# Both output projections of a two-layer decoder trunk as seven half-size products

## The chip, the core and the metric

The kernel runs on one core of a Trainium2 chip. The metric is the device time of one execution in microseconds; the kernel before takes 640.55 us (median of three runs, 639.79 to 640.93). The core has a matrix engine (TensorE, PE in the profile), three engines for elementwise work (VectorE, ScalarE, GpSimd; DVE, ACT and POOL), a queue engine that only issues transfers here (SyncE, SP), a working memory of 128 partitions (SBUF) and eight banks for matmul results (PSUM).

## What is computed

The input x is 512 rows of 1024 numbers, all in float32. Two layers follow one another:

```python
# layer 0: x + mixed @ w_out_e,  mixed = [A(h) * silu(z_A) | B(h) * silu(z_B)],  h = RMSNorm(x)
# layer 1: x + mixed @ w_out_o,  mixed = [C(h) * silu(z_C) | D(h) * silu(z_D)]
mixed = jnp.concatenate([oc.reshape(B, S, C_W) * jax.nn.silu(cz),
                         od.reshape(B, S, D_W) * jax.nn.silu(dz)], axis=-1)
return x + mixed @ w_out
```

A, B, C and D are four kinds of attention with 512 output columns each; q, k, v and z come from one input projection per layer. The output projection is a product of 512x1024 by 1024x1024, and it is this product, once per layer, that is changed.

## The kernel before

Precision: a float32 product is made of three passes of rounded float32 (`F32R`). Each operand is split into a high part (a cast) and a low part (operand minus high part); the passes are high x high, high x low and low x high, and they accumulate in PSUM. So each operand costs one cast and one subtraction ahead of its matmuls.

Weights stream from DRAM in chunks of 256 rows by up to 512 columns (`Weights`, lines 355 to 419): `load` brings a chunk into a `wr` buffer (4 of them), `conv` splits it into `wh` and `wl` (3 each). ScalarE casts the high part; the low part goes to VectorE for chunks of odd number and to GpSimd, in two halves, for even ones. The order of the chunks is the list `chunks` (lines 447 to 470). When a chunk is used up, `done` converts the one three places on and loads the one five places on.

`stream` (line 473) runs one projection: four PSUM banks of tag `proj` (there are four in all), eight K-steps of 128 taken from four chunks. `out_proj` (line 793) is such a stream for the output projection: for each half of the columns, four row blocks of 128, eight K-steps and three passes, 96 matmuls of 128x512, 192 a layer. Its left operand are the gated attention outputs `MA` and `MB`: `gate` makes silu(z) from the z projection (`bz`, `az`, `cz`, `dz`), `gated` multiplies with the attention output `OT` and splits the result into two parts. Layer 0 starts with B's half (K-steps 4 to 7), so that A's last heads and gates may come later; layer 1 starts with C's half. Behind layer 0's projection each row block is added to x, transposed on TensorE and split into the next layer's `hH` and `hL` (`h_block`, line 587), and stored for the residual. The first column half supplies K-steps 0 to 3 of layer 1's first projection, `cqk0`, the second one 4 to 7. Behind layer 1's the sum is stored.

The order of the instructions is worked out ahead of time. The body is recorded as a list of operations; `Plan.schedule` (line 227) places them one by one, always the one that can start soonest by its table of prices, and among those that can start alike the one recorded first, with an advance for operations on `proj` banks (280 places) and on `wr` buffers (230 places) (`key`, line 330). Each tag has a fixed number of buffers (`TAGS`, line 28), given out in the order of recording except for the small ones. Each engine then runs its own list in that order. All transfers of weights, of K copies (`k<-k`) and of results stand in the one queue of SyncE. The planner charges a VectorE operation with two SBUF inputs up to 0.25 us if GpSimd is at work (`SHARED`, line 108). In every stage the projections of the next group serve as filler between the attention's matmuls.

Every operation is emitted by one line (352), so the profile's groups are told apart by tiles: `proj<-wh,k` and `proj<-wl,k` are the output projections' matmuls (`MA` and `MB` lie in `k` buffers, and the weights are the moving operand), `wl<-wr,wh` a weight chunk's low part, `v<-proj,v` the addition to the residual, `hL` the low part of the next layer's input.

## Time and profile before

| what | value |
|---|---|
| median of three runs | 640.55 us |
| profiled execution | 639.81 us, span 638.0 us |
| TensorE busy | 626.2 us (98%) |
| VectorE / ScalarE / GpSimd busy | 444.2 / 379.9 / 292.8 us |
| granted TensorE clock | 1.00 in all stretches |
| DRAM and SBUF transfers | 63.01 MB, mean 99 GB/s |

The span runs from the first to the last instruction. Busy time of TensorE counts matmuls that overlap in its pipeline, so the spacing of matmuls, not their length, says what one costs. Layer 0's output projection lies at 255.6 to 302 us, layer 1's ends the kernel. Times in the rows are us from the span's start unless marked ns; a row's name is output<-inputs.

### The profile page before, as it was taken

To read this page: it belongs to the slowest core of one execution; us is meant where nothing else is said; L and a number is where in the kernel's file an instruction comes from. 1 tells how busy PE (TensorE), PEld (TensorE's weight loads), DVE (VectorE), ACT (ScalarE), POOL (GpSimd) and SP (SyncE) were. 2 spreads that over 40 slices of the span, in tenths; PEclk is the share of its full clock that TensorE was granted. 3 is DMA by queue.
4 is the path that set the end of the run, shared out by engine and by line. 5 is a ranking of instruction groups with operands and counts; after the bars stand their busy time and mean duration, and the time that the engine had idled before them with its cause. 6 is when DMAs were issued, how large, how long until landed. Compare 5 with 4: busy or idle time off the path is not lost.

```text
span 638.0 us, 10566 instructions
## 1 busy us (share of the span) xinstructions
PE 626.2 (98%) x3425; PEld 526.7 (83%) x3425; DVE 444.2 (70%) x1156; ACT 379.9 (60%) x919; POOL 292.8 (46%) x406
## 2 busy tenths in 40 slices
PE   8999999999999999999999999999999999999997
PEld 7788887888888778888887788889998887887786
DVE  4674786987867894652459267688698789898631
ACT  6664785857756664453453266578578677576510
POOL 2543474753374442311363234765478454544310
PEclk9999999999999999999999999999999999999999
DMA  8553215133107123353245431152442102101321
GB/s 290 195 133 99 72 42 154 43 120 101 67 34 228 37 87 112 100 165 99 72 136 156 130 85 36 38 143 62 130 124 75 35 34 83 67 4 64 124 108 66
DMA packets 48126, 63.01 MB, mean 99 GB/s; under 512 B 4664, under 2 KB 29640, under 8 KB 48072
## 3 DMA queue, kind: packets, MB, share of 16 engines
q1 hardware_dynamic: 47896, 62.28, 32.1%
q8 instruction: 27, 0.44, 0.3%
q14 instruction: 27, 0.22, 0.1%
q10 hardware_dynamic: 176, 0.07, 0.1%
HBM read 50.80 MB, written 4.19 MB: 86 GB/s over the span
## 4 chain that ended last, share of the span: by engine, by line
PE 82%; DVE 9%; ACT 3%; issue 2%; DMA 2%; POOL 1%; SPq 0%; DVEq 0%; ACTq 0%; POOLq 0%
PE proj L352 59%; PE tr L352 10%; PE av L352 7%; PE sc L352 6%; DVE p L352 2%; DVE ptl L352 1%; DVE kn L352 1%; DMA wr<-in_w_in_e_dram 1%; DVE k L352 1%; DVE wl L352 1%; DVE sm L352 1%; ACT wh L352 1%; ACT p L352 1%; DMA wr<-in_phi_w_dram 1%; DVE sq L352 1%
## 5 line engine op out<-in xcount | busy, mean ns | idle before, releaser
L352 POOL TENSOR_TENSOR wl<-wr,wh 128x512 fp32r<-128x512 f32 (+2 forms) x87 | 103.3, 1206 | 145.4 <-ACT wh L352 145.2
L352 PE MATMUL proj<-wh,hH 128*128 128x512 f32 (+2 forms) x416 | 152.7, 369 | 1.6 <-DVE kn L352 1.0
L352 PE MATMUL proj<-wl,hH 128*128 128x512 f32 (+2 forms) x416 | 151.8, 366 | 0.0
L352 PE MATMUL proj<-wh,hL 128*128 128x512 f32 (+2 forms) x416 | 150.8, 366 | 0.0
L352 ACT ACTIVATE p<-p,sm 128x128 f32<-128x128 f32 (+3 forms) x160 | 90.0, 563 | 50.0 <-DVE sm L352 46.8
L352 ACT CAST wh<-wr 128x1024 fp32r<-128x1024 f32 (+2 forms) x89 | 83.9, 944 | 55.8 <-PE proj L352 47.4
L352 PEld LDWEIGHTS proj<-wh,hH 128*128 128x128 f32 x416 | 78.3, 189 | 13.0 <-ACT p L352 1.3
L352 PEld LDWEIGHTS proj<-wl,hH 128*128 128x128 f32 x416 | 78.5, 189 | 9.3
L352 PEld LDWEIGHTS proj<-wh,hL 128*128 128x128 f32 x416 | 78.2, 189 | 9.4
L352 PE MATMUL proj<-wh,k 128*128 128x512 f32 x256 | 83.4, 398 | 0.0
L352 DVE CUSTOM_DVE_ANT_0 p<-sc,bias 128x128 f32<-128x128 f32 (+3 forms) x160 | 76.6, 480 | 8.4 <-PE sc L352 5.5
L352 PE MATMUL sc<-k,qq 128*128 128x256 f32 (+3 forms) x304 | 79.3, 338 | 0.9 <-DVE sm L352 0.8
L352 POOL TENSOR_SCALAR p<-p,sm 128x128 f32<-128x128 f32 (+1 forms) x80 | 45.4, 570 | 71.5 <-DVE sm L352 60.6
L352 DVE TENSOR_TENSOR ptl<-tr,pth 128x128 fp32r<-128x128 f32 (+3 forms) x144 | 68.1, 484 | 11.8 <-ACT pth L352 10.3
L352 ACT CAST pth<-tr 128x128 fp32r<-128x128 f32 (+3 forms) x144 | 58.8, 421 | 27.7 <-PE tr L352 26.5
L352 POOL TENSOR_SCALAR p<-p,sm,dg 128x128 f32<-128x128 f32 (+3 forms) x64 | 44.4, 697 | 51.6 <-DVE sm L352 43.5
L352 DVE TENSOR_TENSOR wl<-wr,wh 128x1024 fp32r<-128x1024 f32 (+2 forms) x45 | 51.2, 1138 | 23.4 <-ACT wh L352 23.2
L352 PE MATMUL tr<-ident,p 128*128 128x128 f32 x360 | 62.2, 275 | 1.8 <-POOL p L352 1.2
L352 POOL TENSOR_TENSOR sm<-sm,nhalf 128x8 f32<-128x8 f32 (+3 forms) x53 | 61.9, 1169 | 3.1
L352 PEld LDWEIGHTS sc<-k,qq 128*128 128x128 f32 x304 | 51.4, 189 | 10.6 <-DVE sm L352 3.6
L352 PE MATMUL proj<-hH,wh 128*128 128x512 f32 x144 | 58.5, 407 | 0.4 <-DVE kn L352 0.4
L352 PE MATMUL proj<-hH,wl 128*128 128x512 f32 x144 | 57.7, 401 | 0.0
(148 smaller groups left out, 1103.2 us busy)
## 6 DMA issues: line engine op xcount, KB each, us to landing
wr<-in_w_in_e_dram SPq DMA_DIRECT2D x32, 256.0 KB, 2.8
wr<-in_w_in_e_dram SPq DMA_DIRECT2D x16, 512.0 KB, 4.6
wr<-in_w_in_o_dram SPq DMA_DIRECT2D x28, 256.0 KB, 2.9
k<-k SPq DMA_DIRECT2D x24, 256.0 KB, 3.3
wr<-in_w_in_o_dram SPq DMA_DIRECT2D x12, 512.0 KB, 4.1
wr<-in_w_out_e_dram SPq DMA_DIRECT2D x8, 512.0 KB, 3.6
wr<-in_w_out_o_dram SPq DMA_DIRECT2D x8, 512.0 KB, 3.9
v<-in_x_dram SPq DMA_DIRECT2D x2, 1024.0 KB
```

What stands on the lines that cost most here:

```text
L352: getattr(getattr(self.nc, op.eng), op.method)(*[real(a) for a in op.args], **{k: real(a) for k, a in op.kw.items()})
```

## The change

Each output projection is split into quarters: the left operand (the gated outputs) by row half and K half into A11, A12, A21, A22 (the first index is the row half of 256, the second the K half of 512; K's first half is B's in layer 0, C's in layer 1), the weights into four quarters of 512x512. Seven products of 256x512 by 512x512 (P0 to P6) replace the eight, in the form with S1 = A21 + A22, S2 = S1 - A11, S3 = A11 - A21, S4 = A12 - S2 on the left and four combinations of the weight quarters on the right.

The weight combinations are made by GpSimd (`combinations`): for each layer eight pieces, each with four loads of 128 KB into the one `vc` buffer, four additions or subtractions of 128x256, and four stores to a DRAM tensor (`dram0`, `dram1`). They are recorded behind the first group of B heads. The weight stream then has 14 chunks per projection instead of eight, three products' from `w_out` itself and four from the combinations.

The left operands are split per product (`split_rows`): casts on ScalarE, low parts on VectorE for five products and on GpSimd for S4 and A22. The gates now only multiply into `OT` in place. P3 adds onto P0's two banks and P5 onto P4's; P2 and P6 use the `sc` and `av` banks. Each result is added by VectorE to the two column halves of x to which it belongs (`add`), 20 additions of 128x512 a layer instead of eight, with the last addition of a block followed by `h_block` (layer 0) or the store (layer 1). `cqk0` takes its K-steps in the order 4 to 7, 0 to 3.

```diff
...
         name, pieces, q = self.order[s]
         raw = self.plan.tile("wr", [128, 2, 512])
         c = 0
+        if callable(pieces):
+            self.Y.dma_start(raw, pieces(q))
+            pieces, c = (), 512
...
+    def seven(name, w, wt, late):
+        src = w.rearrange("(kt p) c -> p kt c", p=128)
+        def quarter(k, n):
+            k = 4 * (k ^ late)
+            return lambda u: src[:, k + 2 * u:k + 2 * u + 2, 512 * n:512 * n + 512]
+        def comb(t):
+            return lambda u: wt[:, t, 2 * u:2 * u + 2, :]
+        ops = (quarter(0, 0), comb(2), quarter(1, 0), comb(1), comb(0), quarter(1, 1), comb(3))
+        return [(f"{name}P{n}", op, (0, 1)) for n, op in enumerate(ops)]
+    oeT = st("dram0", [128, 4, 4, 512])
+    ooT = st("dram1", [128, 4, 4, 512])
...
-        ("oe0", [(woe, 0, 512, 1, 0)], QO),
-        ("oe1", [(woe, 512, 512, 1, 0)], QO),
-        ("cqk0", [(wo, 0, 256, 2, 512)], Q4),
+        *seven("oe", woe, oeT, True),
+        ("cqk0", [(wo, 0, 256, 2, 512)], QO),
...
-        ("oo0", [(woo, 0, 512, 1, 0)], Q4),
-        ("oo1", [(woo, 512, 512, 1, 0)], Q4),
+        *seven("oo", woo, ooT, False),
...
+    def combinations(w, wt, late):
+        src = w.rearrange("(kt p) c -> p kt c", p=128)
+        for t in range(4):
+            for c in range(2):
+                b = st("vc", [128, 4, 256])
+                for n in range(4):
+                    kt = t + 4 * ((n // 2) ^ late)
+                    c0 = 512 * (n % 2) + 256 * c
+                    Y.dma_start(b[:, n, :], src[:, kt, c0:c0 + 256])
+                for dst, x, y, op, to in ((3, 3, 1, OP.subtract, 2), (1, 1, 0, OP.subtract, 0), (0, 3, 0, OP.add, 1),
+                                          (2, 0, 2, OP.subtract, 3)):
+                    G.tensor_tensor(out=b[:, dst, :], in0=b[:, x, :], in1=b[:, y, :], op=op)
+                    Y.dma_start(wt[:, to, t, 256 * c:256 * c + 256], b[:, dst, :])
+    def split_rows(dst, src, eng):
+        for c, v in enumerate(src):
+            A.copy(dst[0][:, 2 * c:2 * c + 2, :].bitcast(F32R), v)
+        for c, v in enumerate(src):
+            eng.tensor_sub(dst[1][:, 2 * c:2 * c + 2, :].bitcast(F32R), v, dst[0][:, 2 * c:2 * c + 2, :])
+        return dst
+    def combine(dst, a, b, op):
+        for d, x, y in zip(dst, a, b):
+            V.tensor_tensor(out=d, in0=x, in1=y, op=op)
+        return dst
+    def rows2(tag):
+        return [st(tag, [128, 512]).rearrange("p (c q) -> p c q", c=2) for _ in range(2)]
+    def parts(tag):
+        t = st(tag, [128, 2, 2, 4, 256])
+        return [(t[:, n, 0], t[:, n, 1]) for n in range(2)]
+    def two_parts():
+        return st("pth", [128, 4, 256]), st("ptl", [128, 4, 256])
+    def product(name, banks, rows, fresh=True):
+        for u in range(2):
+            _, wh, wl = W.next(name)
+            for r in range(2):
+                for kk in range(2):
+                    for pi, (w, low) in enumerate(((wh, 0), (wl, 0), (wh, 1))):
+                        T.matmul(banks[r], rows[low][:, 2 * u + kk, 128 * r:128 * r + 128].bitcast(F32R), w[:, kk, :],
+                                 start=fresh and u == 0 and kk == 0 and pi == 0, stop=u == 1 and kk == 1 and pi == 2,
+                                 skip_group_check=not fresh)
+            W.done()
+        return banks
+    def seven_products(name, OT, first, gate_first, gate_second, xs, done):
+        second = 4 - first
+        quad = [[[OT[:, k + 2 * c:k + 2 * c + 2, 256 * r:256 * r + 256] for c in range(2)] for k in (first, second)]
+                for r in range(2)]
+        (A11, A12), (A21, A22) = quad
+        def add(banks, hf, i0, op=OP.add, last=False):
+            for r in range(2):
+                V.tensor_tensor(out=xs[hf][:, i0 + r, :], in0=xs[hf][:, i0 + r, :], in1=banks[r], op=op)
+                if last:
+                    done(i0 + r, hf)
+        def two():
+            return [pt("proj") for _ in range(2)]
+        gate_first()
+        pa11, ps3 = parts("k")
+        split_rows(pa11, A11, V)
+        S3 = combine(rows2("kn"), A11, A21, OP.subtract)
+        split_rows(ps3, S3, V)
+        main = product(name + "P0", two(), pa11)
+        add(main, 0, 0)
+        side = product(name + "P1", two(), ps3)
+        add(side, 0, 2)
+        add(side, 1, 2)
+        gate_second()
+        pa12, ps2 = parts("k")
+        split_rows(pa12, A12, V)
+        S1 = combine(rows2("p"), A21, A22, OP.add)
+        S2 = combine(rows2("p"), S1, A11, OP.subtract)
+        split_rows(ps2, S2, V)
+        p2 = product(name + "P2", [pt("sc"), pt("av")], pa12)
+        ps1 = split_rows(two_parts(), S1, V)
+        add(p2, 0, 0, last=True)
+        product(name + "P3", main, ps2, False)
+        add(main, 1, 2)
+        add(main, 1, 0)
+        add(main, 0, 2)
+        S4 = combine(A11, A12, S2, OP.subtract)
+        side = product(name + "P4", two(), ps1)
+        add(side, 1, 2, last=True)
+        ps4 = split_rows(two_parts(), S4, G)
+        product(name + "P5", side, ps4, False)
+        a22 = st("qq", [128, 2, 4, 256])
+        pa22 = split_rows((a22[:, 0], a22[:, 1]), A22, G)
+        add(side, 1, 0, last=True)
+        p4 = product(name + "P6", [pt("sc"), pt("av")], pa22)
+        add(p4, 0, 2, OP.subtract, last=True)
...
+    combinations(woe, oeT, 1)
+    combinations(woo, ooT, 0)
...
-    acc = proj("bz", hH, hL, 512, True)
-    MB = new_m()
-    gate_now(acc, rb, OT, 4, MB)
-    acc = proj("az", hH, hL, 512, True)
-    gA = gate_later(acc, rb, "qq")
-    MA = new_m()
-    for a in range(4):
-        gated(gA[:, a, :], OT, a, MA)
+    def gate_b():
+        acc = proj("bz", *h0, 512, True)
+        for a in range(4):
+            g = st("sq", [128, 512])
+            gate(acc[a], rb, g)
+            V.tensor_tensor(out=OT[:, 4 + a, :], in0=g, in1=OT[:, 4 + a, :], op=OP.mult)
+        acc = proj("az", *h0, 512, True)
+        gA.append(gate_later(acc, rb, "qq"))
+
+    def gate_a():
+        for a in range(4):
+            V.tensor_tensor(out=OT[:, a, :], in0=gA[0][:, a, :], in1=OT[:, a, :], op=OP.mult)
+
+    def block_done(i, hf):
+        x1 = xs[hf]
+        h_block(x1[:, i, :], i, 4 * hf, gO, hH, hL)
+        sq = st("sq", [128, 512])
+        A.activation(out=sq, in_=x1[:, i, :], func=AF.Square, accum_out=ssh[:, hf, i:i + 1])
+        Y.dma_start(x1d[:, i, hf, :], x1[:, i, :])
     x1d = st("dram", [128, NB, 2, 512])
     ssh = st("ssh", [128, 2, NB])
+    gA, xs = [], []
+    for hf in range(2):
+        xs.append(st("v", [128, NB, 512]))
+        Y.dma_start(xs[hf], x2.rearrange("(i p) c -> p i c", p=128)[:, :, 512 * hf:512 * hf + 512])
+    h0 = hH, hL
     hH, hL = new_h()
-    for hf in range(2):
-        x1 = st("v", [128, NB, 512])
-        Y.dma_start(x1, x2.rearrange("(i p) c -> p i c", p=128)[:, :, 512 * hf:512 * hf + 512])
-        acc = out_proj(f"oe{hf}", MA, MB)
-        for i in range(NB):
-            V.tensor_tensor(out=x1[:, i, :], in0=acc[i], in1=x1[:, i, :], op=OP.add)
-            h_block(x1[:, i, :], i, 4 * hf, gO, hH, hL)
-            sq = st("sq", [128, 512])
-            A.activation(out=sq, in_=x1[:, i, :], func=AF.Square, accum_out=ssh[:, hf, i:i + 1])
-            Y.dma_start(x1d[:, i, hf, :], x1[:, i, :])
+    seven_products("oe", OT, 4, gate_b, gate_a, xs, block_done)
...
-    acc = proj("cz", hH, hL, 512, True)
-    MA = new_m()
-    gate_now(acc, rb, OT, 0, MA)
-    acc = proj("dz", hH, hL, 512, True)
-    gB = gate_later(acc, rb, "v")
-    MB = new_m()
-    for a in range(4):
-        gated(gB[:, a, :], OT, 4 + a, MB)
+    def gate_c():
+        acc = proj("cz", hH, hL, 512, True)
+        for a in range(4):
+            g = st("sq", [128, 512])
+            gate(acc[a], rb, g)
+            V.tensor_tensor(out=OT[:, a, :], in0=g, in1=OT[:, a, :], op=OP.mult)
+        acc = proj("dz", hH, hL, 512, True)
+        gB.append(gate_later(acc, rb, "qq"))
+
+    def gate_d():
+        for a in range(4):
+            V.tensor_tensor(out=OT[:, 4 + a, :], in0=gB[0][:, a, :], in1=OT[:, 4 + a, :], op=OP.mult)
+
+    def store(i, hf):
+        Y.dma_start(out[0, 128 * i:128 * i + 128, 512 * hf:512 * hf + 512], xs[hf][:, i, :])
+
+    gB, xs = [], []
     for hf in range(2):
-        xr = st("v", [128, NB, 512])
-        Y.dma_start(xr, x1d[:, :, hf, :])
-        acc = out_proj(f"oo{hf}", MA, MB)
-        for i in range(NB):
-            V.tensor_tensor(out=xr[:, i, :], in0=acc[i], in1=xr[:, i, :], op=OP.add)
-            Y.dma_start(out[0, 128 * i:128 * i + 128, 512 * hf:512 * hf + 512], xr[:, i, :])
+        xs.append(st("v", [128, NB, 512]))
+        Y.dma_start(xs[hf], x1d[:, :, hf, :])
+    seven_products("oo", OT, 0, gate_c, gate_d, xs, store)
```

## Rows read from the trace of the kernel before

**Rows 1.** The page's first part: the span, and each engine's busy time.
```profile
span 638.0 us, 10566 instructions
...
PE 626.2 (98%) x3425; PEld 526.7 (83%) x3425; DVE 444.2 (70%) x1156; ACT 379.9 (60%) x919; POOL 292.8 (46%) x406
```

**Rows 2.** The page's chain that ended last, by engine and by line.
```profile
PE 82%; DVE 9%; ACT 3%; issue 2%; DMA 2%; POOL 1%; SPq 0%; DVEq 0%; ACTq 0%; POOLq 0%
PE proj L352 59%; PE tr L352 10%; PE av L352 7%; PE sc L352 6%; DVE p L352 2%; DVE ptl L352 1%; DVE kn L352 1%; DMA wr<-in_w_in_e_dram 1%; DVE k L352 1%; DVE wl L352 1%; DVE sm L352 1%; ACT wh L352 1%; ACT p L352 1%; DMA wr<-in_phi_w_dram 1%; DVE sq L352 1%
```

**Rows 3.** Stages: length, then PE, PEld, DVE, ACT, POOL busy, clock, DMA share, GB/s.
```profile
247.50:255.60 8.10, 8.10 (x37) 6.61 (x37) 4.89 (x8) 3.09 (x5) 0.00 (x0) 1.00 0.56 194
255.60:266.60 11.00, 11.00 (x49) 9.00 (x48) 10.31 (x12) 5.11 (x7) 3.00 (x2) 1.00 0.30 99
266.60:277.60 11.00, 11.00 (x48) 8.84 (x47) 2.08 (x3) 4.07 (x8) 2.54 (x2) 1.00 0.51 165
277.60:290.00 12.40, 12.40 (x64) 10.27 (x63) 7.47 (x19) 7.17 (x21) 2.55 (x2) 1.00 0.43 130
290.00:301.90 11.90, 11.90 (x53) 9.58 (x52) 2.21 (x4) 4.19 (x8) 2.55 (x2) 1.00 0.32 109
...
540.00:600.00 60.00, 59.17 (x335) 49.71 (x333) 52.85 (x151) 41.35 (x106) 26.80 (x35) 1.00 0.14 45
600.60:634.30 33.70, 33.63 (x145) 26.70 (x143) 9.91 (x12) 4.35 (x5) 4.88 (x4) 1.00 0.32 117
```

**Rows 4.** The chain in order of time, its last long piece: start, us, what.
```profile
604.20 30.08 PE proj L352 x129
```

**Rows 5.** Groups of TensorE by shape: count, busy us, mean ns, idle before.
```profile
L352 PE MATMUL proj<-wh,k 128*128 128x512 f32 x256 | 83.4, 398 | 0.0
...
L352 PE MATMUL proj<-wl,k 128*128 128x512 f32 x128 | 50.5, 395 | 0.0
```

**Rows 6.** Timeline of TensorE where the heads end: start, us, what.
```profile
246.70 0.28 PE L352 MATMUL av<-ptl,v 128*128 128x128 f32 x1
...
255.58 0.39 PE L352 MATMUL proj<-wh,k 128*128 128x512 f32 x1
...
600.58 0.39 PE L352 MATMUL proj<-wh,k 128*128 128x512 f32 x1
```

**Rows 7.** Timeline of VectorE in layer 0's output projection.
```profile
255.56 1.23 DVE L352 TENSOR_TENSOR wl<-wr,wh 128x1024 fp32r<-128x1024 f32 x1 [0.45 <-ACT wh L352]
256.70 0.69 DVE L352 TENSOR_TENSOR kn<-proj,rb 128x512 f32<-128x512 f32 x1
257.30 1.45 DVE L352 TENSOR_TENSOR kn<-qq,ot 128x512 f32<-128x512 f32 x1
258.68 1.78 DVE L352 SCALAR_TENSOR_TENSOR qq<-qq,kn 128x512 f32<-128x512 f32 x1
...
269.63 0.69 DVE L352 TENSOR_TENSOR v<-proj,v 128x512 f32<-128x512 f32 x1 [3.64 <-PE proj L352]
...
280.15 2.16 DVE L352 SCALAR_TENSOR_TENSOR hL<-tr,lncol,hH 128x128 fp32r<-128x128 f32 x8 [0.56 <-ACT hH L352]
```

**Rows 8.** Timeline of GpSimd in the same stretch.
```profile
256.91 3.00 POOL L352 TENSOR_TENSOR wl<-wr,wh 128x512 fp32r<-128x512 f32 x2 [10.22 <-ACT wh L352]
268.01 2.54 POOL L352 TENSOR_TENSOR wl<-wr,wh 128x512 fp32r<-128x512 f32 x2 [8.10 <-ACT wh L352]
```

**Rows 9.** Timeline of ScalarE in the same stretch.
```profile
262.83 1.05 ACT L352 CAST wh<-wr 128x1024 fp32r<-128x1024 f32 x1
264.29 0.62 ACT L352 CAST k<-kn 128x512 fp32r<-128x512 f32 x1 [0.41 <-DVE kn L352]
```

**Rows 10.** The page's DMA issues: count, KB each, median us to landing.
```profile
wr<-in_w_out_e_dram SPq DMA_DIRECT2D x8, 512.0 KB, 3.6
...
wr<-in_w_in_o_dram SPq DMA_DIRECT2D x16, 128.0 KB, 2.2
```

**Rows 11.** Groups of GpSimd by shape: count, busy us, mean ns, idle before.
```profile
L352 POOL TENSOR_TENSOR wl<-wr,wh 128x256 fp32r<-128x256 f32 x16 | 11.9, 766 | 14.1 <-ACT wh L352 14.1
```

More of the change, by code (lines that the diff above doesn't have):

```diff
@@ L27 @@
 LOOSE = ("tr", "sm1", "sm2", "sm4", "sm8", "sm16", "sm64")
-TAGS = {"proj": 4, "sc": 1, "tr": 2, "av": 1, "dram": 1,
+TAGS = {"proj": 4, "sc": 1, "tr": 2, "av": 1, "dram": 1, "dram0": 1, "dram1": 1,
         "wr": 4, "wh": 3, "wl": 3, "qq": 2, "k": 2, "v": 2, "pth": 2, "ptl": 2, "hH": 1, "hL": 1, "ot": 1,
@@ L198, in price @@
             out = writes[0] if writes else reads[0]
-            local = writes and reads and all(r.root.tag not in ("dram",) for r in (writes[0], reads[0]))
+            local = writes and reads and all(not r.root.tag.startswith("dram") for r in (writes[0], reads[0]))
             rate = 270.0 if local else 330.0 if out.shape[-1] >= 256 else 180.0
@@ L340, in emit @@
     def emit(self, order, sb, ps, dr):
-        pools = {"dram": dr}
+        pools = {t: dr for t in ("dram", "dram0", "dram1")}
         pools.update({t: ps for t in PSUM_TAGS})
```

## The prediction

> **What bounds the kernel now.** I read the page's first part, then the chain of waits, then the table of stages, and last the timelines of each engine at the two output projections. The first part shows TensorE busy 626.2 of 638.0 us [rows 1]; the chain that ended last is 82% TensorE, 59% of the span being matmuls into `proj` [rows 2]. So a matmul less is worth its spacing, as long as the others can still feed TensorE. The stage table says where they can: in the four windows of layer 0's projection (255.6 to 301.9) VectorE is busy 10.31 + 2.08 + 7.47 + 2.21 = 22.1 of 46.3 us and the granted clock is 1.00; in the 60 us before layer 1's projection VectorE is busy 52.85 of 60 us; in the last 33.7 us only 9.91 [rows 3].
>
> **What is removed.** The spacing of these matmuls is in the chain's last long piece: 129 in 30.08 us, 0.233 us each; the window 255.6 to 266.6 has 49 in 11.00 us [rows 3, 4]. I take 0.23. The projections are 256 + 128 = 384 matmuls [rows 5], 192 a layer. Seven products of 2 K-steps x 2 row blocks x 2 x 3 = 24 make 168. Removed: 2 x 24 x 0.23 = 11.0 us, all on the path if nothing new waits.
>
> **What is added in layer 0.** The last attention matmul there is at 246.70 and the first projection matmul at 255.58 [rows 6]: from 246.7 on TensorE has only `az`, then the products, so no other work covers a stall until `cqk0`. Seven products last 168 x 0.23 = 38.6 us, 5.5 each. Prices on VectorE, as start to start: a 128x512 operation 0.60 (256.70 to 257.30), a weight chunk's low part 1.14 (255.56 to 256.70), an `hL` piece 2.16/8 = 0.27 [rows 7]. Each product eats two weight chunks, so VectorE makes one low part per product. Its demand, product by product:
> P0: last `az` block 3, S3 and its low part 4 (S3's `kn` buffers come free only behind the `az` gates): 7 x 0.60 + 1.14 = 5.3.
> P1: P0's additions 2, A12's low part 2, S1 and S2 4: 8 x 0.60 + 1.14 = 5.9.
> P2: P1's additions 4, low parts of S2 and S1 4: 5.9.
> P3: P2's additions 2, S4 2, `hL` 8 x 0.27: 4 x 0.60 + 2.2 + 1.14 = 5.7.
> P4: P3's additions 6: 4.7. P5 and P6: additions 2 and `hL` 8 each: 4.5.
> Sum 36.5 of 38.6 us, against 22.1 of 46.3 now. It fits only just, and up to P3 it does not: 22.8 asked of 22.1. P3 waits for S2's low part, which comes last of its queue; what queues behind it is P1's additions, which P4's banks wait for. If every operation came at its price the stall would be under 1 us.
> It will not. GpSimd makes the other low parts, and while it did so from 256.91 to 259.91 (3.00 us for two against 2.54 at 268.01) [rows 8], VectorE's two operations with both inputs in SBUF took 1.45 and 1.78 us instead of 0.69, 1.85 more together; an addition from PSUM stayed at 0.69 [rows 7]. The new stage has 7 such GpSimd pairs and 4 single low parts (S4 and A22), nine pairs in all. If a third of them meet VectorE's two-input work, as they do now only where VectorE is dense, that is 9 x 1.85 / 3 = 5.6 us more: 36.5 + 5.6 - 38.6 = 3.5 us of stall. Bounds: 0, since the additions can drift later than the combinations, and 9 x 1.85 + 36.5 - 38.6 = 14.6 if all meet. I take 3.5, near the row of dense work.
> The Trainium skill (SBUF — State Buffer, Who interferes with whom) says that a VectorE instruction with two SBUF inputs and a GpSimd instruction reading SBUF exclude one another, whoever started first keeping the port for the whole instruction, and that one with a single SBUF input is not touched. The trace agrees on both halves (1.78 against 0.69, and 0.69). Taken as the price of every pair it makes the slow rival below.
> ScalarE: 14 weight casts of 1.05 and 14 half-row copies of 0.62 [rows 9] are 23.4 us beside the squares and `hH` that it has already; no term. Weights: 512 KB per 2.75 us; one lands in 3.6 us [rows 10] and loads are issued five chunks, 13 us, ahead; no term, bounds 0 to 2.
> P5 adds onto P4's banks, so it waits for P4's additions; the first bank is complete six matmuls (1.4 us) before the second, an addition takes 0.69, so this only just hides. No term, bounds 0 to 1.4. At the end `cqk0` starts with the half that P4 and P5 complete; P6 (5.5 us) covers that `hL`, and 48 matmuls (11 us) cover the last rows. Nothing.
>
> **What is added in layer 1.** The first matmul after the last D head is at 600.58 [rows 6], and 145 matmuls follow from there [rows 3]: 47 of the 48 that need only C's half were already used as filler among the heads. There is no filler left over, so what delays the last head delays the end. VectorE, 88% busy there, gets 6 operations (low parts of A11 and S3, and S3) and 4 additions (P0, half of P1), and loses 7 low parts: +3 x 0.60, and one weight low part of 1.14: 2.9 us. Bounds: 0 (it idles 7 us in that window [rows 3]) and 6 (with every pair met). I take 2.5, since VectorE is nearly full. After the last head P2 to P6 are 120 matmuls, 27.6 us, against 13 operations, 16 additions and 4 low parts, 29 x 0.60 + 4.6 = 22 us: no term, bounds 0 to 3. The residual's second half now loads alone once the last V buffer is free and is wanted only by P4's banks, 11 us later.
>
> **The combinations.** 64 GpSimd additions and subtractions of 128x256; the like row takes 766 ns [rows 11]: 49 us, in 16 groups, one buffer, each of four loads (128 KB: 2.2 us [rows 10]), four chained operations, four stores. By these rows a group is some 2.2 + 4 x 0.77 + a store like the load, 7.5 us, an estimate of 10 with queueing: 160 us, while layer 0's are wanted at 255. They sit among the layer-0 heads. Cover: the 8.9 us of `az` that now run after the last head, which would move forward as filler. SyncE's queue gets 128 more DMAs, the stores waiting for GpSimd with weight loads and K copies behind them. The first groups' loads also fall into the start, where the weight loads are. Bounds 0 to 3; I take 0.5, nearer to the covered end because of those 8.9 us.
>
> **Sum.** 11.0 - 3.5 - 2.5 - 0.5 = 4.5 us less than the profiled execution's 639.81, which is 0.74 under the median 640.55: 636.0 on the median.
>
> **Rivals.**
> A, nothing new waits: stalls of 0 to 2 us, 630 to 631.5. For it: VectorE's 36.5 us fit, and the order is worked out ahead of time. Against it: P0 to P3 are over full even without contention.
> B, the forecast, 631.5 to 639.2.
> C, VectorE takes over as the bound of the layer-0 stage and eats all: stalls of 9.5 to 12 us, 639 to 641.8. It needs about two thirds of the pairs to meet.
> D, the shared port, on the other side: every GpSimd pair costs VectorE its 1.85 us. Layer 0's stage is then 36.5 + 16.7 = 53 us, less some 3 that may slide under `cqk0`, 50 against the 192 x 0.23 = 44.2 now: 6 us lost; in layer 1's end 22 + 6 x 1.85 = 33 against 27.6, so 5.5 - 5.5 = 0, and the heads' 2.5. 640.55 + 8.5 = 649. It decides from 11 us of stall. Against it: VectorE's additions, 20 of a layer's operations, read one SBUF operand and do not meet.
> E, the combinations come late, or their stores block SyncE's queue ahead of weight loads: only if a group took 28 us; that is not seen in any row, and I put it into D's chance.
>
> **Chances.** A 0.17, B 0.55, C 0.13, D and E 0.15. Two runs of this kernel differ by some 0.2%, 1.3 us, so faster means under 639.3: A and B, 0.72; same 0.12; slower 0.16. The range leaves out 0.08 at the bottom and about 0.12 at the top: 630.5 to 642.5; the forecast alone, 631.5 to 639.2.
>
> **What would show it.** 336 matmuls instead of 384 at 0.23 us; TensorE idle of some 3 to 4 us between P0 and P4 of layer 0 with VectorE as what ended it; VectorE over 85% busy there, two-input operations at 1 us and more; the last D head 2 to 3 us later relative to TensorE's matmuls before it; GpSimd's 64 at about 0.77 us and done well before 250 us. Wrong if the idle stands at `wh` or `wl` (weights too late), at a DMA, or at the start of the kernel; or if TensorE stays gapless and the time falls by 10.

## The result and the profile after

The changed kernel takes 657.56 us (median of four runs, 656.40 to 658.99) against 640.26 for the kernel before, now also of four runs: a ratio of 1.0273, 95% interval 1.0257 to 1.0289. Forecast were 636.0 and a range up to 642.5. The prediction was wrong, and in direction too: 17.3 us lost where 4.5 were to be won.

The profiled execution took 656.59 us. Its page: the span, busy times, and the chain that ended last by engine and by line.
```profile
span 654.6 us, 10944 instructions
...
PE 627.3 (96%) x3377; PEld 516.7 (79%) x3377; DVE 493.0 (75%) x1206; ACT 399.5 (61%) x943; POOL 382.2 (58%) x490
...
PE 47%; DVE 14%; POOL 13%; issue 6%; DMA 4%; ACT 4%; SPq 1%; POOLq 0%; DVEq 0%; ACTq 0%
```
48 matmuls are gone, as planned (3425 to 3377 [rows 1]). But the chain that was 82% TensorE [rows 2] is now 47%, and GpSimd, 1% of it before, has 13%.

The heads of layer 0 before (columns as in [rows 3]).
```profile
20.00:255.58 235.58, 233.89 (x1211) 192.78 (x1210) 175.97 (x464) 150.76 (x366) 118.63 (x165) 1.00 0.32 99
```
The stages of the changed kernel: the heads of layer 0, the products of layer 0 up to `cqk0`'s first matmul, the end of layer 1 behind the last D head, and three short stretches inside them.
```profile
20.00:265.64 245.64, 238.92 (x1212) 190.65 (x1211) 183.10 (x463) 151.97 (x367) 173.90 (x231) 1.00 0.52 164
...
265.64:316.83 51.19, 45.13 (x197) 34.76 (x196) 47.20 (x72) 31.71 (x65) 28.26 (x18) 0.97 0.53 170
...
265.64:276.00 10.36, 8.40 (x34) 5.77 (x32) 10.36 (x10) 5.11 (x7) 7.90 (x5) 1.00 0.34 104
...
278.00:280.00 2.00, 2.00 (x6) 1.59 (x5) 2.00 (x5) 1.14 (x2) 0.13 (x1) 0.50 0.68 231
...
616.00:654.60 38.60, 31.44 (x122) 23.26 (x121) 26.06 (x31) 11.75 (x16) 15.42 (x11) 0.94 0.41 136
624.00:626.00 2.00, 2.00 (x6) 1.52 (x6) 1.97 (x5) 0.00 (x0) 0.00 (x0) 0.52 0.29 75
```
VectorE is busy 7.1 us more among the heads with about the same operations (183.10 against 175.97). In layer 0's projection, where it was busy 22.1 us before [rows 3], it is busy 47.20 of 51.19 us, and at the stage's start without a gap (10.36 of 10.36).

TensorE's timeline at the products: the last layer-0 head, the first product matmul, and its longer waits, with what ended them.
```profile
256.75 0.28 PE L352 MATMUL av<-ptl,v 128*128 128x128 f32 x1
...
265.64 0.39 PE L352 MATMUL proj<-wh,k 128*128 128x512 f32 x1
...
277.29 0.85 PE L352 MATMUL proj<-wh,k 128*128 128x512 f32 x2 [2.38 <-DVE k L352]
...
287.39 0.50 PE L352 MATMUL proj<-wl,k 128*128 128x512 f32 x1 [1.08 <-POOL wl L352]
...
290.78 0.73 PE L352 MATMUL proj<-wh,k 128*128 128x512 f32 x2 [0.32 <-DVE k L352]
...
303.47 0.66 PE L352 MATMUL tr<-ident,v 128*128 128x128 f32 x4 [1.40 <-DVE v L352]
...
622.39 1.15 PE L352 MATMUL sc<-wh,k 128*128 128x512 f32 x2 [1.24 <-DVE k L352]
```

VectorE in the same stretch, and GpSimd beside it.
```profile
268.45 1.78 DVE L352 TENSOR_TENSOR kn<-ot 128x512 f32<-128x512 f32 x1
270.15 1.78 DVE L352 SCALAR_TENSOR_TENSOR qq<-qq,kn 128x512 f32<-128x512 f32 x1
271.85 0.68 DVE L352 TENSOR_TENSOR ot<-qq,ot 128x512 f32<-128x512 f32 x1
272.46 0.68 DVE L352 TENSOR_TENSOR v<-v,proj 128x512 f32<-128x512 f32 x1
273.05 1.91 DVE L352 TENSOR_TENSOR wl<-wr,wh 128x1024 fp32r<-128x1024 f32 x1
274.89 0.67 DVE L352 TENSOR_TENSOR v<-v,proj 128x512 f32<-128x512 f32 x1
275.49 1.15 DVE L352 TENSOR_TENSOR kn<-ot 128x512 f32<-128x512 f32 x1
276.56 1.45 DVE L352 TENSOR_TENSOR k<-kn,k 128x512 fp32r<-128x512 f32 x2
...
287.80 2.32 DVE L352 TENSOR_TENSOR wl<-wr,wh 128x1024 fp32r<-128x1024 f32 x1
```
```profile
267.48 3.90 POOL L352 TENSOR_TENSOR wl<-wr,wh 128x512 fp32r<-128x512 f32 x2 [1.23 <-ACT wh L352]
...
272.61 3.49 POOL L352 TENSOR_TENSOR wl<-wr,wh 128x512 fp32r<-128x512 f32 x2 [1.23 <-ACT wh L352]
```
Read the two side by side. While GpSimd works on a weight chunk (267.48 to 271.38), VectorE's operations with both inputs in SBUF take 1.78 us instead of 0.68; between two such chunks (271.85) they take 0.68; the addition from a PSUM bank takes 0.67 also in the middle of a chunk (274.89); and GpSimd's pair itself takes 3.90 and 3.49 instead of 2.54 [rows 8].

The longest wait, 2.38 us, is P1's. It is for S3's low part: S3 lies in `kn` buffers, its second half is summed at 275.49, and `k<-kn,k` at 276.56 is the subtraction that releases TensorE. P3 waits only 0.32 us for S2's low part (290.78), after 1.08 us for a weight chunk's low part (287.39).

Four marks split the span: the first product (or projection) matmul, `cqk0`'s first, the last D head's matmul, and the end. Before they stand at 255.58, 302.63, 599.96 and 638.0, after at 265.64, 316.83, 615.71 and 654.6, so the pieces are 255.58, 47.05, 297.33 and 38.04 us before and 265.64, 51.19, 298.88 and 38.89 after. The losses are 10.06 among layer 0's heads, 4.14 in its products, 1.55 in layer 1's heads and 0.85 at the end: 16.6, the difference of the spans. As each set of products has 24 matmuls less, 5.5 us, the second and the fourth take 9.6 and 6.4 us more than the matmuls left in them would need at the old pace.

### The profile page after: what moved, and what is told of

It is laid out like the page before. It is cut to its first block, busy times and chain, and to the rows that moved or that the text cites. A ratio compares the mean times of both kernels' runs of the same rounds, so it can differ in the third digit from the quotient of the medians.

```text
span 654.6 us, 10944 instructions
## 1 busy us (share of the span) xinstructions
PE 627.3 (96%) x3377; PEld 516.7 (79%) x3377; DVE 493.0 (75%) x1206; ACT 399.5 (61%) x943; POOL 382.2 (58%) x490
## 4 chain that ended last, share of the span: by engine, by line
PE 47%; DVE 14%; POOL 13%; issue 6%; DMA 4%; ACT 4%; SPq 1%; POOLq 0%; DVEq 0%; ACTq 0%
PE proj L352 28%; PE tr L352 7%; PE av L352 7%; PE sc L352 5%; POOL vc L352 4%; POOL sm L352 3%; POOL p L352 3%; POOL wl L352 3%; DVE wl L352 3%; DVE p L352 2%; DVE v L352 2%; DMA dram<-vc 2%; DVE ot L352 1%; DMA vc<-in_w_out_o_dram 1%; DVE kn L352 1%
## 5 line engine op out<-in xcount | busy, mean ns | idle before, releaser
L352 POOL TENSOR_TENSOR wl<-wr,wh 128x512 fp32r<-128x512 f32 (+2 forms) x99 | 125.2, 1282 | 105.8 <-ACT wh L352 91.2
L352 ACT CAST wh<-wr 128x1024 fp32r<-128x1024 f32 (+2 forms) x101 | 96.5, 957 | 58.0 <-PE proj L352 42.9
L352 DVE TENSOR_TENSOR ptl<-tr,pth 128x128 fp32r<-128x128 f32 (+3 forms) x144 | 67.6, 484 | 11.3 <-ACT pth L352 10.1
L352 DVE TENSOR_TENSOR wl<-wr,wh 128x1024 fp32r<-128x1024 f32 (+2 forms) x51 | 62.8, 1233 | 17.0 <-ACT wh L352 16.8
L352 POOL TENSOR_SCALAR p<-p,sm,dg 128x128 f32<-128x128 f32 (+3 forms) x64 | 46.4, 728 | 46.1 <-DVE sm L352 40.3
L352 POOL TENSOR_SCALAR p<-p,sm 128x128 f32<-128x128 f32 (+1 forms) x80 | 48.3, 607 | 41.4 <-DVE sm L352 36.4
L352 PEld LDWEIGHTS tr<-ident,p 128*128 128x128 f32 x360 | 43.2, 140 | 22.8 <-POOL p L352 13.5
```

What stands on the lines that cost most here:

```text
L352: getattr(getattr(self.nc, op.eng), op.method)(*[real(a) for a in op.args], **{k: real(a) for k, a in op.kw.items()})
```

## Experiments

The theory after reading: the loss is contention. VectorE and GpSimd exclude each other where an operation of each reads two tiles from SBUF (below, "the port" stands for this exclusion), and the change adds GpSimd's reads both among the heads (combinations) and where VectorE is newly full (products). Rivals: the combinations' transfers and SyncE's queue; the order around the one `vc` buffer; a chain of dependences through the left sums; plain load on VectorE; the weight chain through ScalarE's casts.

Every edit has the whole order worked out anew, so pieces of the span that it doesn't touch can move too. The four marks are therefore given where the total alone would mislead.

**The two halves of the change alone.** One run keeps the products and drops the combinations, the other keeps the old projections and adds the combinations.
```diff
-            return lambda u: wt[:, t, 2 * u:2 * u + 2, :]
+            return quarter(t // 2, t % 2)
...
-    combinations(woe, oeT, 1)
-    combinations(woo, ooT, 0)
...
```


> The changed kernel without the combinations: no loads, no GpSimd operations, no stores; the weight stream reads plain quarters of w_out in their place, so everything from the first product on is as in the changed kernel. In the changed kernel the first product's matmul stands at 265.64 us against 255.58 before. Theory (the combinations among layer 0's heads cost this): first product at 255 to 256 us, 647 to 648 us in all. Rival (the products' own preparation, gates and splits ahead of the first product, costs it): still near 265 us, 655 or more.

Measured: 648.04 us, 1.0103 (1.0074 to 1.0132). The four pieces of its span are 256.40, 51.10, 299.31 and 38.89: 9.2 of the heads' 10.1 us are gone, the products' losses are all there. So the seven products lose to the eight even when the combinations of their weights cost nothing.

The combinations added to the kernel before:
```diff
...
+    combinations(woe, oeT, 1)
+    combinations(woo, ooT, 0)
```


> The kernel before, with the combinations added at the same place and their result not used; the projections are the old ones. Theory: layer 0's projection starts at 264 to 266 us instead of 255.6, 650 us in all. Rival (the combinations only hurt together with the products): 640 to 642 us.

Measured: 651.58 us, 1.0161 (1.0125 to 1.0198); the first projection matmul comes at 264.46, and the pieces behind it are those of the kernel before to 0.1 us. The halves lose 7.4 and 10.9 us and together 17.3, so they nearly add up; the four runs of this kernel go from 648.74 to 653.36.

**What of the combinations costs.** First the transfers alone, then the order around the buffer, then fills, which write the same pieces without reading, in the place of the additions.
```diff
-                    G.tensor_tensor(out=b[:, dst, :], in0=b[:, x, :], in1=b[:, y, :], op=op)
```


> The changed kernel with the combinations' 64 GpSimd operations left out; their loads and stores stay, so the products read uncombined weights. If the transfers and SyncE's queue are the cost: 656 to 658 us, first product near 265 us. If GpSimd is the cost, by waiting or by working: 647 to 649 us, first product near 256 us.

Measured: 650.68 us, 1.0151 (1.0129 to 1.0173), the first product at 258.35. Against 648.04 without any, loads and stores cost 2.6 us; GpSimd's 64 operations cost 6.9 more (657.56).

```diff
-                op.end = dma_free + 1600.0
+                op.end = dma_free + (5600.0 if [r.tag for r in op.roots] == ["vc"] else 1600.0)
```


> The changed kernel, same work, with one number of the planner changed: it takes the combinations' loads to land 4 us later than it did, so that GpSimd's list has other work in front of the operations that wait for them. Theory (GpSimd's fixed order stands still behind a load that is later than planned, 10.9 us of idle right ahead of the combinations' operations in the profile): 648 to 653 us, that idle under 4 us. Rival (GpSimd's time and the shared port, 64 operations of 0.81 us): 656 to 660 us.

Measured: 660.59 us, 1.0300 (1.0270 to 1.0331). As the main cause this theory fell. GpSimd's idle time ahead of the combinations went from 10.9 to 2.9 us, as the edit meant, and the kernel got slower. But the run isn't a clean test: the first product came 2.3 us earlier (263.32), while eight of the 64 operations now ran inside layer 0's products (from 273.93 to 308.10), whose stage took 52.93 us in place of 51.19, and layer 1's heads took 301.29 in place of 298.88. So some of the heads' loss may have been this idle time, or may only have moved. The groups of GpSimd, first of the change, then of this run:
```profile
L352 POOL TENSOR_TENSOR vc<-vc 128x256 f32<-128x256 f32 x64 | 51.8, 809 | 10.9 <-DMA vc<-in_w_out_e_dram 4.4 <-DMA vc<-in_w_out_o_dram 3.9
```
```profile
L352 POOL TENSOR_TENSOR vc<-vc 128x256 f32<-128x256 f32 x64 | 55.0, 859 | 2.9 <-DMA vc<-in_w_out_o_dram 0.4
```

```diff
-                    G.tensor_tensor(out=b[:, dst, :], in0=b[:, x, :], in1=b[:, y, :], op=op)
+                    for _ in range(2):
+                        G.memset(b[:, dst, :], 0.0)
```


> The changed kernel with each of the combinations' 64 GpSimd operations replaced by two fills of the same 128x256 piece: nearly the same GpSimd time (some 0.6 instead of 0.8 us), priced alike by the planner, but nothing read from SBUF; loads and stores stay, the result is not the reference's. With no GpSimd operation it was 650.7 us, with the operations 657.6. Theory (the port that GpSimd shares with VectorE is the cost): 650 to 652.5 us. Rival (GpSimd's time, which pushes back the heads' own GpSimd work): 655 to 658 us.

Measured: 650.95 us, 1.0156 (1.0139 to 1.0172), 0.3 above the run with transfers only. The fills, and the heads of layer 0 in this run, to be held against the heads' row of the changed kernel above:
```profile
L354 POOL MEMSET vc<- 128x256 f32 x128 | 35.3, 311 | 19.4 <-DMA vc<-in_w_out_e_dram 11.6 <-issue 3.4 <-DMA vc<-in_w_out_o_dram 3.3
...
20.00:258.52 238.52, 234.93 (x1212) 193.30 (x1211) 176.71 (x464) 150.42 (x367) 153.87 (x295) 1.00 0.56 169
```
So 35.3 us of GpSimd's time without reading cost 0.3 us, and 51.8 us with reading 6.6 more. The fills are 16.5 us shorter in sum, which no run tests apart; but it is VectorE's own busy time that falls, by 6.4 us for the same work (176.71 against 183.10), and the stretch is 7.1 us shorter. That speaks for the reading.

The first product's time splits the same loss without the rest of the kernel: 256.40 without combinations, 258.35 with their transfers, 258.52 with fills, 265.64 with the additions, that is 1.95, 0.17 and 7.12 us. One reason why the medians differ from this is the end of layer 1: these edits don't touch it, and in the profiled runs it takes 41.51 and 41.25 us with transfers only and with fills against 38.89 in the other two, at a granted clock of 0.91 in place of 0.94. So a split by medians is good to some 2.5 us, an estimate from these ends.

**What of the products costs.** All from the kernel without combinations (648.04).

The sums S1 to S4 and their splits left out (P1 and P4 then read A11's parts, P3 and P5 A12's; the result lacks the sums):
```diff
-        S3 = combine(rows2("kn"), A11, A21, OP.subtract)
-        split_rows(ps3, S3, V)
+        ps3 = pa11
...
```


> The changed kernel without the weight combinations (648.0 us) and also without the sums S1 to S4 and their splits; the products take the split of A11 or A12 in their place. Per layer this leaves out 8 VectorE sums, 6 low parts on VectorE, 2 on GpSimd and 8 casts; matmuls, weights and additions stay. Theory (the chain gate, sum, cast, low part in front of each product on VectorE stalls TensorE): most of the 17 us of stalls in both projection stages goes, 634 to 640 us. Rival (the 20 additions from PSUM, which come first in VectorE's list): 645 us or more.

Measured: 630.91 us, 0.9836 (0.9816 to 0.9857): 17.1 us less. That takes away load, chain and meetings at once; the next runs part them.

Of the additions, only the eight last ones of a layer:
```diff
-        add(main, 0, 0)
-        add(side, 0, 2)
-        add(side, 1, 2)
...
-        add(main, 1, 2)
-        add(main, 1, 0)
-        add(main, 0, 2)
```


> The changed kernel without the weight combinations (648.0 us), with only the last addition of each block kept: 8 a layer instead of 20, the sums stay; the result lacks the products left out. If the additions are what crowds VectorE: 636 to 641 us. If the sums and splits are: 645 to 648 us.

Measured: 642.34 us, 1.0026 (1.0015 to 1.0036). Layer 0's stage without combinations, and then with eight additions:
```profile
256.40:307.50 51.10, 45.04 (x197) 34.79 (x196) 47.10 (x72) 31.65 (x65) 28.16 (x18) 0.97 0.53 170
```
```profile
255.03:305.53 50.50, 44.69 (x197) 35.23 (x196) 42.65 (x60) 31.71 (x65) 26.60 (x18) 0.97 0.55 172
```
VectorE's busy time fell by 4.5 us and the stage by 0.6; 4.0 us came from the end of layer 1 (38.89 to 34.86). So in layer 0 it isn't the additions' load: VectorE's additions from PSUM can go almost without effect, and TensorE's longest wait for VectorE's `k` is then 3.97 us.

The sums computed, but unread by the products:
```diff
-        side = product(name + "P1", two(), ps3)
+        side = product(name + "P1", two(), pa11)
...
-        product(name + "P3", main, ps2, False)
+        product(name + "P3", main, pa12, False)
...
```


> The changed kernel without the weight combinations (648.0 us); S1 to S4 are summed and split as in it, but P1, P3, P4 and P5 read the splits of A11 and A12 instead, so that no product waits for a sum; the result is not the reference's. VectorE's and GpSimd's load are unchanged, the chain sum, cast, low part, product is cut. Without sums and splits altogether it was 630.9 us. If the chain's length is the cost: 631 to 637 us. If the load is: 644 to 648 us.

Measured: 642.83 us, 1.0040 (1.0028 to 1.0052), and layer 0's stage 50.57 us in place of 51.10. Nor is it the chain through the sums by itself: freed of it, TensorE waits for other results of VectorE, at the longest 3.04 us for `v`.

```diff
-        S3 = combine(rows2("kn"), A11, A21, OP.subtract)
+        S3 = combine(rows2("p"), A11, A21, OP.subtract)
```


> The changed kernel without the weight combinations (648.0 us), same work, with S3 in p buffers instead of kn buffers, so that S3 need not wait behind the az and dz gates for a buffer. In layer 0 P1 waits 2.4 us for S3's low part, and the granted clock is at half behind that for some 4 us. If the buffer order makes that wait: 643 to 645 us and no half clock in layer 0. If VectorE's load makes it: 647 to 648.5 us.

Measured: 650.13 us, 1.0146 (1.0127 to 1.0166), above both bands. Its two stages, layer 0's and the end of layer 1:
```profile
255.96:304.32 48.36, 42.92 (x197) 33.92 (x196) 44.02 (x68) 30.03 (x63) 26.85 (x18) 1.00 0.58 180
603.46:647.60 44.14, 33.94 (x131) 25.37 (x130) 29.95 (x34) 12.82 (x16) 16.75 (x11) 0.92 0.38 131
```
The total hides two changes. In layer 0 the wait for S3's low part is gone, the clock is 1.00, and the stage is 2.7 us shorter (48.36 against 51.10): there S3's buffers do cost time. At the end of layer 1 the new order loses 5.3 us (44.14 against 38.89), with a wait of 3.35 us for VectorE's `k`; why was not tested.

Then GpSimd's reads in the product stages replaced by fills:
```diff
+                    if "P" in self.order[s][0]:
+                        for _ in range(2):
+                            self.G.memset(lo[:, k, :n].bitcast(F32), 0.0)
...
+            if eng is G:
+                for _ in range(2):
+                    G.memset(dst[1][:, 2 * c:2 * c + 2, :], 0.0)
```


> The changed kernel without the weight combinations (648.0 us), with GpSimd's low parts in the two projection stages (7 weight chunks of 2 halves a layer, and those of S4 and A22) replaced by two fills of the same 128x512 piece each: nearly the same GpSimd time, priced alike, but nothing read from SBUF; the result is not the reference's. Theory (in the stages too the shared port stretches VectorE's two-input sums and low parts from 0.69 to 1.7 us): 636 to 641 us. Rival (VectorE's work is too much even at its own price, or the chain too long): 645 to 648 us.

Measured: 630.52 us, 0.9853 (0.9832 to 0.9874), 17.5 less. But such a fill waits neither for the weights nor for ScalarE's cast, so the run also shortened the weight chain. The next run puts a one-column subtraction ahead of the fills, which waits for both:
```diff
+                        self.G.tensor_sub(lo[:, k, :1], raw[:, k, :1], hi[:, k, :1].bitcast(F32))
                         for _ in range(2):
                             self.G.memset(lo[:, k, :n].bitcast(F32), 0.0)
...
+                G.tensor_sub(dst[1][:, 2 * c:2 * c + 2, :1].bitcast(F32R), v[:, :, :1], dst[0][:, 2 * c:2 * c + 2, :1])
                 for _ in range(2):
                     G.memset(dst[1][:, 2 * c:2 * c + 2, :], 0.0)
```


> Plain quarters instead of combinations, as in the run without combinations (648.0 us), and GpSimd's low parts in the two product stages replaced by two fills each, but with a one-column subtraction ahead of every pair of fills that reads the weight buffer and its cast, so that GpSimd waits for ScalarE exactly as in the change. It leaves out the values of these low parts. Theory (the shared port makes the stalls of the stages): 630 to 633 us, first product at about 255, two-input operations of VectorE at 0.68 us. Rival (the fills won by not waiting for the casts, that is, the weight chain was the stall): 640 us or more, with waits of TensorE for wl.

Measured: 632.42 us, 0.9870 (0.9854 to 0.9887). So 15.6 us of the 17.5 are regained without touching that wait, and the weight chain holds at most 1.9. By the marks of the profiled runs (16.1 us between their spans), 8.0 are in layer 0's stage, 5.3 at the end, and 2.8 among the heads. Its page, its two stages (the second from behind the last D head), and VectorE in the first:
```profile
span 629.6 us, 10697 instructions
```
```profile
254.53:297.59 43.06, 42.50 (x198) 33.96 (x196) 38.25 (x71) 31.11 (x65) 23.66 (x48) 1.00 0.65 202
597.00:629.60 32.60, 27.19 (x114) 21.11 (x114) 21.45 (x31) 11.52 (x15) 12.33 (x27) 1.00 0.42 146
```
```profile
256.47 0.69 DVE L354 TENSOR_TENSOR kn<-ot 128x512 f32<-128x512 f32 x1
257.08 0.68 DVE L354 SCALAR_TENSOR_TENSOR qq<-qq,kn 128x512 f32<-128x512 f32 x1
...
259.48 1.22 DVE L354 TENSOR_TENSOR wl<-wr,wh 128x1024 fp32r<-128x1024 f32 x1
```
The same operations that took 1.78 and 1.91 us take 0.68 and 1.22. VectorE's work is 38.25 us in place of 47.20 and fits into 43.06; TensorE is busy 42.50 of them at full clock. In this run, too, S3 lies in `kn`, and P1 doesn't wait: in these runs the buffers cost time only together with the port.

As a control, the kernel before with the same fills in its output projections:
```diff
+                    if self.order[s][0][:2] in ("oe", "oo"):
+                        for _ in range(2):
+                            self.G.memset(lo[:, k, :n].bitcast(F32), 0.0)
...
```


> The kernel before with GpSimd's low parts of the output projections' weight chunks (two chunks of two halves in each layer's eight that it makes) replaced by two fills each; it leaves out the values of those low parts. Theory (the price of the port belongs to the new stages, where VectorE is full): VectorE's two operations at 257 to 260 us go back to 0.69, the time stays within 1.5 us of the kernel before, 639 to 640.5. Rival (the fills take away a cost that the kernel before pays as well, so the 17.5 us are not the change's): 634 us or less.

Measured: 639.60 us, 0.9985 (0.9976 to 0.9995). There, too, VectorE's two stretched operations [rows 7] go back to 0.68 and 0.69, beside fills:
```profile
258.02 0.68 DVE L354 TENSOR_TENSOR kn<-qq,ot 128x512 f32<-128x512 f32 x1
258.80 0.69 DVE L354 SCALAR_TENSOR_TENSOR qq<-qq,kn 128x512 f32<-128x512 f32 x1
```
It is worth about 1 us (640.75 against 639.60): the price belongs to the new stages, in which VectorE has no slack.

**Both together, and a remedy that isn't one.** The whole change with both kinds of fills (the two edits above in one kernel):


> The whole change, with its transfers, with both kinds of fills: GpSimd's 64 combinations and its low parts in the product stages write without reading (behind the one-column subtraction that waits for the cast). It leaves out the values of the combinations and of these low parts. Theory (the loss is transfers 2.6 us and the port for the rest): 632 to 635 us, faster than the kernel before. Rival (some other part of the change costs time beside the port, such as VectorE's queue or the banks' order): 640 us or more.

Measured: 636.55 us, 0.9934 (0.9909 to 0.9959), 21.0 under the change, by 1.5 above the expected band.
```profile
span 635.0 us, 11032 instructions
...
PE 617.7 (97%) x3377; PEld 517.6 (82%) x3377; DVE 471.8 (74%) x1206; ACT 397.0 (63%) x943; POOL 358.6 (56%) x626
```
Over the run with the products' fills alone (632.42) it has 4.1 us where transfers and fills gave 2.9; the other 1.2 are within the interval of this run (1.6 us to either side).

The planner charged more for a meeting:
```diff
-SHARED = 250.0
+SHARED = 1000.0
```


> The changed kernel in full (657.6 us), same work, with the planner's cap on what GpSimd may cost a two-input VectorE operation raised from 0.25 to 1.0 us. If the loss comes from lists made in a wrong order because of that price: 648 to 654 us. If it comes from the work itself meeting at the port: 656 to 660 us.

Measured: 661.14 us, 1.0326 (1.0302 to 1.0349), slower than the change itself. At this price the order moves the loss and raises it: layer 0's products and the end of layer 1 are shorter than in the change (50.50 and 36.12 us against 51.19 and 38.89), but the first product comes at 270.74, 5.1 us later, and layer 1's heads take 301.94 us in place of 298.88. No kernel that computes the whole result and beats the one before was found.

## Why the prediction was wrong

The removed work came as said: 48 matmuls, 11.0 us. The four costs set against it were 0.5, 3.5, 2.5 and 0; measured, in the same order, 10.1, 9.6, 1.6 and 6.4. Their sum less the saving, 27.6 - 11.0, is the 16.6 us between the spans.

**The combinations, 0.5 (bounds 0 to 3): the step that failed most, by 9.6 us.** Of the 10.1 us, 0.8 stay when the combinations go (256.40 against 255.58); 9.2 are theirs. Two assumptions broke. GpSimd's operations were priced by their own time and SyncE's queue, though [rows 7] stood there to price them by what they do to VectorE; the 64 were never put into the contention sum, which counted only the product stages. Their reading costs 6.6 us and their transfers 2.6 by the medians, 7.1 and 2.0 by the first product's time. And the cover wasn't there: "the 8.9 us of `az`" were to move forward as filler. The lists are fixed ahead; the last head came 10.05 us later (256.75 against 246.70), and `az` still takes 8.89 us behind it, as before (8.88). Each engine runs its own list in order, so work that stands later in it didn't fill gaps that arose in front. Of rival E, the transfers have a small share; the first and last of the combinations ran at 26.91 and 244.00 us, 217 us from first to last in place of the estimated 160, but before they are wanted.

**Layer 0's stage, 3.5 (bounds 0 to 14.6): mechanism right in the main, size and place off.** VectorE's own demand was worked out as 36.5 us; with fills in place of GpSimd's reads it is 38.25. Contention was taken as a third of the pairs meeting, 5.6 us; VectorE's busy time grew by 9.0 (47.20 - 38.25). It was also treated as a sum of VectorE's time alone. GpSimd's pairs are stretched as well (28.26 us busy with the pairs, 23.66 with the fills), so `wl` comes late too (1.08 us at 287.39). And the wait stood elsewhere: the forecast put it at P3, for S2's low part, where 0.32 us were measured; the 2.38 us stand at P1, for S3's low part, and matmuls at a granted clock of 0.50 followed. The prediction says that S3's `kn` buffers come free late, and gave that no price; with S3 in other buffers the stage was 2.7 us shorter. Of its signs, VectorE over 85% busy (92%) and two-input operations of 1 us and more came; TensorE's idle time in the stage is 6.1 us, not 3 to 4. The argument used against rival D, that additions from PSUM don't meet, is true (0.68 us), and the run with eight additions shows why it didn't help: in layer 0 those were not the operations that TensorE waited for longest.

**Layer 1's heads, 2.5 (0 to 6):** 1.6 measured, so the size was right. Its parts were not tested one by one; with fills in place of the products' GpSimd reads 1.1 is left (298.41 against 297.33).

**Behind the last head, "no term, bounds 0 to 3":** 6.4. The working had 22 us of VectorE in 27.6. With the fills it is 21.45, so the demand was right; contention adds 4.6 (26.06), and a wait of 1.24 us there is again followed by about half the clock. The six pairs of that end were priced for rival D only (6 x 1.85 = 11), and not in the forecast.

Rival D had the mechanism and a chance of 0.15 with E, but nothing for the combinations: with their measured 10.1, its 649 would have been 659.

The sum by the medians: 632.4 with the products and fills in place of GpSimd's reads; + 15.6 port, 13.3 of it in the two stages = 648.0; + 2.6 transfers = 650.7; + 0.3 GpSimd's fills; + 6.6 port under the combinations = 657.6.

The Trainium skill (SBUF — State Buffer, Who interferes with whom) says that a VectorE instruction with two SBUF inputs contends with a GpSimd instruction that reads SBUF, not with one that only writes it. The runs agree: VectorE's operations take 1.78 us beside a reading GpSimd and 0.68 beside fills, and the fills in place of the combinations regain 6.6 us.

## What to carry to other kernels

Price an operation added to GpSimd by what it does to VectorE's two-input operations wherever both run, also where GpSimd looks idle: here fills in place of the combinations cost 0.3 us, while GpSimd's reads cost 6.6 there and 15.6 with the products. A product scheme that trades matmuls for elementwise sums should be costed in every stretch that it touches with the neighbour's contention in, since 11 us of matmuls saved were worth 8.3 with fills and no combinations (632.42) and 4 with the transfers and fills (636.55), in kernels that leave out a part of the result, and a loss of 17.3 in full. In a list that is ordered ahead of time, filler that stands later in the list covered no delay. And when an edit reorders the whole program, compare the stages and not only the total: a gain of 2.7 us in layer 0 lay hidden under a loss of 5.3 in layer 1.

## Not expected of the hardware

The granted clock, 1.00 in all stages shown of the kernel before, fell to 0.50, the lower level of 1.2 GHz, behind TensorE's wait of 2.38 us (278 to 280), which came after two shorter ones of 0.25 and 0.62, and to 0.52 behind one of 1.24 (624 to 626), which came after one of 0.39. From 277.29 to 281.27 ten matmuls took 3.98 us, 0.40 each in place of 0.23: some 1.7 us more, paid after the wait itself. The length of one wait doesn't settle it. Behind the 1.40 us at 303.47 no such fall is seen; nor behind the same 1.24 us, again after a short one of 0.38, in the run with transfers only; nor behind 2.81 us in the run with S3 in other buffers. The wait and the stretch behind it, first of the one, then of the other:
```profile
614.84 0.73 PE L352 MATMUL sc<-wh,k 128*128 128x512 f32 x2 [1.24 <-DVE k L352]
616.00:618.00 2.00, 1.86 (x9) 1.19 (x7) 1.97 (x4) 1.01 (x2) 0.00 (x0) 1.00 0.14 10
```
```profile
274.09 0.50 PE L352 MATMUL sc<-wl,k 128*128 128x512 f32 x1 [2.81 <-DVE wl L352]
276.00:278.00 2.00, 2.00 (x10) 1.59 (x10) 2.00 (x4) 1.43 (x2) 0.10 (x1) 1.00 0.86 266
```
What decides it stays open here.

The exclusion goes both ways. In the kernel with all fills a one-column GpSimd subtraction spans 266.28 to 270.42 in the trace, while VectorE ran operations with two SBUF inputs one behind the other; it ended as the additions from PSUM began:
```profile
266.28 4.14 POOL L356 TENSOR_TENSOR wl<-wr,wh 128x1 fp32r<-128x1 f32 x1 [2.35 <-ACT wh L356]
```
```profile
266.07 1.28 DVE L356 TENSOR_TENSOR k<-kn,k 128x512 fp32r<-128x512 f32 x2
267.27 0.68 DVE L356 TENSOR_TENSOR ot<-qq,ot 128x512 f32<-128x512 f32 x1
267.88 0.68 DVE L356 TENSOR_TENSOR ptl<-p,pth 128x512 fp32r<-128x512 f32 x1
268.48 0.68 DVE L356 TENSOR_TENSOR p<-ot 128x512 f32<-128x512 f32 x1
269.08 0.68 DVE L356 TENSOR_TENSOR k<-ot,k 128x512 fp32r<-128x512 f32 x1
269.68 0.68 DVE L356 TENSOR_TENSOR p<-p,ot 128x512 f32<-128x512 f32 x1
270.29 2.64 DVE L356 TENSOR_TENSOR v<-v,proj 128x512 f32<-128x512 f32 x4
```
GpSimd isn't always kept out so long: in the changed kernel its pair at 267.48 got in between VectorE's operations, and VectorE's operation at 268.45 took 1.78 us. Waits such as the 4.14 us make the low parts late in the fills' runs as well, so some of the port's price is still in their 632.42 and 636.55.
